# Down projection of the feed-forward layers: one Strassen level of seven products, activations stationary, sums made by adding DMAs, the stage in a fixed order

## The chip, the cores and the metric

The kernel is one program on one core of a Trainium2 chip. The metric is the device time of one execution in microseconds, as the median of several runs. The core's engines are called PE (matrix multiplication; PEld is its loading of the stationary operand), DVE, ACT and POOL; SP issues DMAs. POOL issues DMAs too, and all DMAs that add to what already stands in SBUF go through its queue.

## The reference

A two-layer encoder trunk on 512 tokens of width 1024: layer 0 mixes tokens by dilated window attention, layer 1 by gated linear attention (GLA), and each is followed by a feed-forward layer (SwiGLU) of hidden width 2816. The change is in the second product of that layer.

```python
def swiglu(h, w_gate_up, w_down):
    g, u = jnp.split(h @ w_gate_up, 2, axis=-1)
    return (jax.nn.silu(g) * u) @ w_down
...
for i in range(DEPTH):
    hn = rms_norm(h, attn_norm[i])
    ...
    h = h + mix.astype(h.dtype)
    h = h + swiglu(rms_norm(h, ffn_norm[i]), ffn_w_gate_up[i], ffn_w_down[i]).astype(h.dtype)
```

## The kernel before

All values are float32. Each operand of a product is split into a high part in a reduced format (`ACT` copies it) and the low remainder (`DVE` subtracts), and a product is three matmuls: high by high, high by low, low by high (`split`, L92; `mm3`, L106; `product`, L317). The residual h lies in eight tiles of 128 features by 512 tokens.

Gate-up (`gate_up`, L332) goes over six column chunks j, each of 512 gate and 512 up columns (the last 256), by one Strassen level in Winograd's form: seven products of half the size in each direction. Activations are stationary. The weight sums come from `forms` (L236): `load` on SP brings a block, and `add` (L249) issues an adding DMA on POOL. The chunk's results are turned by DVE (`turn`), stored to DRAM by `put` (L352, POOL; the last chunk on SP) in rows of tokens, and read back two chunks later as 22 tiles of 128 hidden features by 512 tokens (`get`, L361, SP). Eight of these tiles take the buffers of h, so h is stored to DRAM at j = 0 (L438) and read back at the end (L494).

The down projection (`down_part`, L471; `down`, L483) is the plain product: for each of eight output tiles m, 22 blocks of hidden features, weights stationary and the 512 tokens moving, three matmuls each. `weight` (L100) streams the weights of a tile in three pieces (1024, 1024 and 768 columns) through two `wf` buffers on SP, splits them, and PE takes 24 or 18 matmuls from each piece. The activations are split once (`halves`) and stay. As each m is done, L497 adds it to h, and `enter_norm` (L143) makes the operands of the next mixer. A little of m = 0 is started inside gate-up.

Outside `manual_schedule` the scheduler orders the instructions by program order and priorities. Each engine and each DMA queue then runs its own list in order, waiting at an instruction for the semaphores of what it needs. Buffers of a tag rotate (`BASE`, `FFN`, `MIX`: `wf` 2, `wh` 3, `wl` 3, `wA` 4, `wB` 2, `sh` 4, `sl` 4, `g` 7, `xs` 16); a new tile waits for the readers of the one whose place it takes. Behind the feed-forward layer of layer 0 comes GLA, whose first products (`linear`, L548, and the product of the gate ranks, L929) take the eight operands `self.x[k]` in order.

## Time and profile before

| | us |
|---|---|
| median of 3 runs | 1476.37 (1473.48 to 1476.51) |
| span of the profiled execution | 1475.3 |
| PE busy | 1449.8 (98% of the span) |
| DVE, ACT, POOL busy | 992.6, 756.1, 162.7 |
| down projection of layer 0, first to last matmul of L108 to L110 in one run | 785.6 to 904.8 |
| the same in layer 1 | 1352.2 to 1471.3 |
| loads of 512 KB, issue to landing: down weights on SP; gate-up weights on SP; gate-up adds and loads on POOL | 3.7; 5.0; 6.1 to 6.4 |
| moved by DMA | 219.61 MB, mean 149 GB/s |

The profiled execution's own time is given by its span, 1475.3 us from its first to its last instruction; the timed runs of the same kernel lie within 1.8 us of that. The views used are the page (busy times, 40 slices), the stretches (busy time of every engine between two times, with the DMA engines' share and rate), the timeline, the groups of instructions by line, and the DMA queues by stretch. q1 hardware_dynamic is what SP issues, q0 software_dynamic what POOL issues; the share is the time that the packets took on the 16 engines.

### The profile page before, as it was taken

Reading aid. Unit: us, or ns where it says so; the run is one execution under the profiler, and the core shown is the slowest. Engines: PE = TensorE matmul, PEld = TensorE weight load, DVE = VectorE, ACT = ScalarE, POOL = GpSimd, SP = SyncE. Lnnn points to the kernel's source line nnn. Section 1 sums busy time; section 2 is a strip of 40 time slices with the busy share of each in tenths; the row PEclk is TensorE's granted clock in tenths of the full one; section 3 lists DMA queues with packets and bytes.
Section 4 is the critical chain, followed back from the end, with each engine's and each line's share of the span. In section 5 each row is a group of like instructions: output and inputs, shape, how many; then the busy total and the mean of one; then the engine's idle time right before and its main releaser. Section 6 shows DMA issues by size and latency. Waiting matters only on the chain.

```text
span 1475.3 us, 20977 instructions
## 1 busy us (share of the span) xinstructions
PE 1449.8 (98%) x7742; PEld 1184.5 (80%) x7742; DVE 992.6 (67%) x1808; ACT 756.1 (51%) x1292; POOL 162.7 (11%) x272
## 2 busy tenths in 40 slices
PE   8999999999999999999999999999999999999998
PEld 6877878787778888877787887888888777778887
DVE  6586868778678669877676435756667876669322
ACT  6344444545566747655565324555745755556221
POOL 0001020101100021122230000000010122221000
PEclk9999999999999999999999999999999999999999
DMA  8644443454433365788887333212264788788431
GB/s 275 183 134 109 104 123 108 109 180 93 131 94 101 87 190 154 195 218 214 220 222 210 95 101 103 86 45 84 71 189 125 229 215 208 208 182 250 143 104 61
DMA packets 99831, 219.61 MB, mean 149 GB/s; under 512 B 15216, under 2 KB 42416, under 8 KB 99728
## 3 DMA queue, kind: packets, MB, share of 16 engines
q1 hardware_dynamic: 81072, 158.35, 34.5%
q0 software_dynamic: 18656, 59.91, 19.1%
q8 instruction: 61, 1.00, 0.3%
q14 instruction: 42, 0.34, 0.1%
HBM read 185.64 MB, written 19.99 MB: 139 GB/s over the span
## 4 chain that ended last, share of the span: by engine, by line
PE 66%; DVE 10%; issue 10%; DMA 7%; ACT 5%; POOL 1%; SPq 1%; DVEq 0%; POOLq 0%; ACTq 0%
PE ppp L110 9%; PE ppp L109 9%; PE ppp L108 9%; PE ppp L570 6%; PE ppp L571 6%; PE ppp L572 6%; PE ppp L329 3%; PE ppp L328 3%; PE ppp L330 3%; DVE wl L97 3%; DMA wA<-in_gate_up_last_dram 2%; DMA wB<-in_gate_up_dram 2%; PE po L701 2%; ACT wh L96 1%; PE ps L661 1%
## 5 line engine op out<-in xcount | busy, mean ns | idle before, releaser
L96 ACT ACTIVATE wh<-wf 128x1024 fp32r<-128x1024 f32 (+1 forms) x184 | 191.4, 1041 | 317.6 <-PE ppp L109 174.6
L97 DVE TENSOR_TENSOR wl<-wf,wh 128x1024 fp32r<-128x1024 f32 (+1 forms) x184 | 219.9, 1196 | 187.1 <-ACT wh L96 186.6
L570 PE MATMUL ppp<-wh,xs 128*128 128x512 f32 (+1 forms) x672 | 258.2, 385 | 7.2 <-ACT wh L96 5.7
L571 PE MATMUL ppp<-wl,xs 128*128 128x512 f32 (+1 forms) x672 | 257.3, 383 | 0.1
L572 PE MATMUL ppp<-wh,xs 128*128 128x512 f32 (+1 forms) x672 | 257.0, 383 | 0.0
L570 PEld LDWEIGHTS ppp<-wh,xs 128*128 128x128 f32 x672 | 126.8, 189 | 36.4 <-ACT wh L96 5.7
L572 PEld LDWEIGHTS ppp<-wh,xs 128*128 128x128 f32 x672 | 126.8, 189 | 25.6 <-issue 1.2
L571 PEld LDWEIGHTS ppp<-wl,xs 128*128 128x128 f32 x672 | 127.1, 189 | 24.8 <-DVE wl L97 0.9
L96 ACT ACTIVATE wh<-wA 128x1024 fp32r<-128x1024 f32 x88 | 93.2, 1059 | 73.4 <-PE ppp L330 27.3
L97 DVE TENSOR_TENSOR wl<-wA,wh 128x1024 fp32r<-128x1024 f32 x88 | 107.4, 1220 | 22.4 <-ACT wh L96 22.2
L329 PE MATMUL ppp<-wl,a 128*128 128x512 f32 (+1 forms) x288 | 108.1, 375 | 1.0 <-DVE wl L97 0.5
L328 PE MATMUL ppp<-wh,a 128*128 128x512 f32 (+1 forms) x288 | 108.4, 377 | 0.1
L108 PE MATMUL ppp<-xs,wh 128*128 128x512 f32 x272 | 106.5, 392 | 0.0
L109 PE MATMUL ppp<-xs,wh 128*128 128x512 f32 x272 | 106.5, 393 | 0.0
L110 PE MATMUL ppp<-xs,wl 128*128 128x512 f32 x272 | 106.0, 391 | 0.0
L330 PE MATMUL ppp<-wh,a 128*128 128x512 f32 (+1 forms) x288 | 105.5, 372 | 0.0
L97 DVE TENSOR_TENSOR wl<-wB,wh 128x1024 fp32r<-128x1024 f32 x38 | 46.5, 1223 | 78.2 <-ACT wh L96 78.2
L649 ACT ACTIVATE sm<-sm,st 128x160 f32<-128x160 f32 (+2 forms) x128 | 56.9, 446 | 43.5 <-DVE st L648 43.4
L329 PE MATMUL ppp<-wl,sh 128*128 128x512 f32 (+1 forms) x192 | 72.8, 379 | 4.6 <-DVE wl L97 4.4
L328 PE MATMUL ppp<-wh,sh 128*128 128x512 f32 (+1 forms) x192 | 71.9, 375 | 2.5 <-ACT g L379 1.8
L330 PE MATMUL ppp<-wh,sl 128*128 128x512 f32 (+1 forms) x192 | 71.6, 373 | 0.0
L251 POOL DMA_DIRECT2D wA<-in_gate_up_dram x44 | 38.5, 874 | 298.9 <-DVE wl L97 210.1
(319 smaller groups left out, 2949.0 us busy)
## 6 DMA issues: line engine op xcount, KB each, us to landing
wA<-in_gate_up_dram POOLq DMA_DIRECT2D x52, 512.0 KB, 6.1
wf<-in_down_dram SPq DMA_DIRECT2D x32, 512.0 KB, 3.7
wf<-in_gate_up_dram SPq DMA_DIRECT2D x24, 512.0 KB, 5.0
wf<-in_a_w_v_dram SPq DMA_DIRECT2D x20, 512.0 KB, 3.8
wB<-in_gate_up_dram POOLq DMA_DIRECT2D x20, 512.0 KB, 6.4
turned<-g POOLq DMA_DIRECT2D x80, 128.0 KB, 6.3
wf<-in_a_w_q_dram SPq DMA_DIRECT2D x16, 512.0 KB, 3.9
zq<-zs SPq DMA_DIRECT2D x128, 64.0 KB, 2.1
```

Source lines behind the costliest of these rows:

```text
L96: nc.scalar.activation(hi, src, AF.Copy)
L97: self.low = nc.vector.tensor_sub(lo, src, hi.bitcast(F32))
L108: mm(out, lhsT=wh, rhs=xh, start=start, stop=False)
L109: mm(out, lhsT=wh, rhs=xl, start=False, stop=False)
L110: self.multiplied = mm(out, lhsT=wl, rhs=xh, start=False, stop=stop)
L328: mm(a, lhsT=xh[:, tok], rhs=wh[:, f], start=start and k == 0, stop=False, skip_group_check=True)
L329: mm(a, lhsT=xh[:, tok], rhs=wl[:, f], start=False, stop=False, skip_group_check=True)
L330: self.multiplied = mm(a, lhsT=xl[:, tok], rhs=wh[:, f], start=False, stop=k == last, skip_group_check=True)
L570: mm(a, lhsT=xh, rhs=wh[:, f], start=k == 0, stop=False)
L571: mm(a, lhsT=xh, rhs=wl[:, f], start=False, stop=False)
L572: self.multiplied = mm(a, lhsT=xl, rhs=wh[:, f], start=False, stop=k == KT - 1)
L649: nc.scalar.activation(sm[:, w], sm[:, w], AF.Exp, bias=n, scale=-1.0, accum_out=l)
```

## The change

The down projection becomes seven products of half the size in each direction. A product has 256 tokens (two stationary tiles of 128), 512 output features (moving) and 1408 hidden features; the hidden features go in six blocks q, five of 256 and one of 128. A block's matmuls are an `item`: 2 token tiles x 2 (or 1) x 3. `ORDER` lists the 42 steps (product, q).

The weight operands are block 0, 1 and 3 of the down weights for products 1, 2 and 3, each streamed through `wf`; for products 5, 6 and 4 a chain tile (`wA`, `wB`) that starts as block 0 and has blocks 2, 3 and 1 added to it in turn; for product 7 block 3 plus block 2 (`sh`, `sl`). Loads are issued on SP, all additions on POOL as adding DMAs. The activation operands come from the turned results in DRAM in the same way: single quarters for 1, 2 and 4; the tile S (`g`), one quarter with three added in turn, for 5, 6 and 3; two quarters for 7. `gated` and `token_norm` give two of the four quarters the opposite sign in gate-up, by twice as many multiplications of half the width, so that all sums are additions. Every product's block of weights and of activations is split anew.

Products are collected in PSUM and in `g` tiles (`finished`), turned back by PE (`turned_back`: eight transposes into two banks and four DVE operations for a quarter of the output) and added to or subtracted from h, which now stays in SBUF. The output's last quarter comes after product 4; h 4 to 7 are complete earlier than h 0 to 3, and GLA's first products and the output take them first (`READY`). The stage stands in `manual_schedule`: `when` puts each DMA at a step, weights are split two steps ahead, activations four.

```diff
-        nc.vector.tensor_scalar(r[:, 4:8], r[:, 0:4], -1.0, None, op0=ALU.mult)
+        for half, sign in ((slice(0, 64), -1.0), (slice(64, P), 1.0)):
+            for c in (4, 8):
+                nc.vector.tensor_scalar(r[half, c:c + 4], r[half, 0:4], sign if c == 4 else -sign, None, op0=ALU.mult)
...
-        self.kept = self.dr.tile([KT, P, S], F32, name=f"h_dram_{layer}")
...
-        def get():
-            c = len(acts)
-            if c < min(4 * (j - 1), NH):
-                a = self.t("h") if c < KT else late[c - KT]
-                nc.sync.dma_start(a, turned[c].rearrange("b i a e -> (b i) (a e)"))
-                acts.append(a)
+        def fetch(p):
+            if j > 1:
+                self.raw[p, j - 2] = self.acts_block(self.t("xs", (P, 2, 256)), *self.FIRST[p], j - 2, nc.sync)
+
+        def gated(e, i, r, g):
+            half = width // 2
+            for n in range(2):
+                f = slice(n * half, (n + 1) * half)
+                col = 4 + 4 * n + i
+                DVE.scalar_tensor_tensor(e[:, f], e[:, f], r[:, col:col + 1], g[:, f], op0=ALU.mult, op1=ALU.mult)
...
-                DVE.scalar_tensor_tensor(e, e, R[:, 4 + i:5 + i], g1[:, i, 0:width], op0=ALU.mult, op1=ALU.mult)
+                gated(e, i, R, g1[:, i, 0:width])
...
-            if j == 0:
-                with self.tc.issue_after(self.added.ins):
-                    for m in range(KT):
-                        nc.gpsimd.dma_start(self.kept[m], self.h[m])
+            if j == 5:
+                self.down_start(layer)
...
+    FIRST = {1: (0, 0), 2: (0, 1)}
+    ORDER = ([(1, q) for q in range(5)] + [(2, q) for q in range(5)] + [(1, 5), (2, 5)]
+             + [(p, q) for p in (5, 6, 3, 7, 4) for q in range(6)])
+
+    def acts_block(self, tile, t, half, q, queue, add=False):
+        c = 4 * q + 2 * half if q < 5 else 20 + half
+        n = 2 if q < 5 else 1
+        src = self.turned_dram[c:c + n, :, :, 2 * t:2 * t + 2].rearrange("c b i a e -> (b i) c (a e)")
+        if add:
...
+    def down_block(self, tile, block, q, queue, add=False):
+        src = self.ins["down"][self.layer, block, q] if q < 5 else self.ins["down_last"][self.layer, block]
+        if add:
...
+    def split_weights(self, p, q):
+        w = self.wraw.pop((p, q)) if p in (1, 2, 3, 7) else self.chain[q]
+        c = 1024 if q < 5 else S
+        self.wpair[p, q] = self.split(w[:, 0:c], (P, c), "wh", "wl")
+
+    def split_acts(self, p, q):
+        nc = self.nc
+        n = 2 if q < 5 else 1
+        raw = self.raw.pop((p, q)) if p in (1, 2, 7, 4) else self.S[q]
+        raw = raw[:, 0:n]
+        hi, lo = (self.t("a", (P, 2, 256), F32R) for _ in range(2))
+        sign = -1.0 if p in (2, 6) else 1.0
+        nc.scalar.activation(hi[:, 0:n], raw, AF.Copy, scale=sign)
+        nc.vector.scalar_tensor_tensor(lo[:, 0:n], raw, sign, hi[:, 0:n].bitcast(F32), op0=ALU.mult, op1=ALU.subtract)
+        self.apair[p, q] = hi, lo
+
+    def stream(self, p, q):
+        self.wraw[p, q] = self.down_block(self.t("wf", (P, 1024)), {1: 0, 2: 1, 3: 3}[p], q, self.nc.sync)
+
...
+        for n in range(3):
+            self.stream(*order[n])
+        for n in range(3):
+            self.split_acts(*order[n])
+            if n < 2:
+                self.split_weights(*order[n])
+
+    def item(self, acc, p, q, tiles, start, stop):
+        mm = self.nc.tensor.matmul
+        (hi, lo), (wh, wl) = self.apair[p, q], self.wpair[p, q]
+        n = 2 if q < 5 else 1
+        for i in tiles:
+            tok = slice(i * P, (i + 1) * P)
+            for k in range(n):
+                f = slice(k * S, (k + 1) * S)
+                xh, xl = hi[:, k, tok], lo[:, k, tok]
+                mm(acc[i], lhsT=xh, rhs=wh[:, f], start=start and k == 0, stop=False, skip_group_check=True)
+                mm(acc[i], lhsT=xh, rhs=wl[:, f], start=False, stop=False, skip_group_check=True)
+                mm(acc[i], lhsT=xl, rhs=wh[:, f], start=False, stop=stop and k == n - 1, skip_group_check=True)
...
+        def chain_load(q):
+            self.chain[q] = self.down_block(self.t("wA" if q < 4 else "wB", (P, 1024)), 0, q, nc.sync)
+
+        def chain_add(q, block):
+            self.down_block(self.chain[q], block, q, nc.gpsimd, True)
+
+        def third_load(q):
+            self.wraw[7, q] = self.down_block(self.t("sh" if q < 4 else "sl", (P, 1024)), 3, q, nc.sync)
+
+        def third_add(q):
+            self.down_block(self.wraw[7, q], 2, q, nc.gpsimd, True)
...
+        def sum_load(q):
+            if q % 2 == 0:
+                rooms.append(self.t("g", (P, 2, 2, 256)))
+            self.S[q] = rooms[-1][:, q % 2]
+            self.acts_block(self.S[q], 1, 0, q, nc.gpsimd)
+
+        def sum_add(q, t, half):
+            self.acts_block(self.S[q], t, half, q, nc.gpsimd, True)
...
+        when(0, raw_load, 1, 4, 0, 0, nc.gpsimd)
+        when(2, raw_load, 2, 4, 0, 1, nc.gpsimd)
+        when(4, raw_load, 1, 5, 0, 0, nc.sync)
+        when(4, raw_load, 2, 5, 0, 1, nc.sync)
+        for n in range(3, len(order)):
+            if order[n][0] in (1, 2, 3):
+                when(n - 4, self.stream, *order[n])
+        for q in range(6):
+            when(at[5, q] - 10, chain_load, q)
+            when(at[5, q] - 8, chain_add, q, 2)
+            when(at[5, q] - 1, chain_add, q, 3)
+            when(at[6, q] - 1, chain_add, q, 1)
+            when(at[7, q] - 9, third_load, q)
+            when(at[7, q] - 7, third_add, q)
+            when(q + 1 if q < 4 else q + 3, sum_load, q)
+            when(q + 2 if q < 4 else q + 4, sum_add, q, 1, 1)
+            when(at[5, q] - 3, sum_add, q, 0, 0)
+            when(at[6, q] - 3, sum_add, q, 0, 1)
+            when(at[7, q] - 9, raw_load, 7, q, 0, 0, nc.sync)
+            when(at[7, q] - 7, raw_add, 7, q, 1, 0)
+            when(at[4, q] - 8, raw_load, 4, q, 1, 1, nc.sync)
+        splits = [[] for _ in order]
+        for n in range(2, len(order)):
+            splits[n - 2].append(partial(self.split_weights, *order[n]))
+        for n in range(3, len(order)):
+            splits[max(n - (2 if order[n] == (1, 4) else 4), 0)].append(partial(self.split_acts, *order[n]))
...
+        def turned_back(tile, half, t, sign):
+
+            for b, tag in enumerate("to"):
+                bank = self.p(tag)
+                for e in range(2):
+                    for i in range(2):
+                        c = slice((2 * b + e) * P, (2 * b + e + 1) * P)
+                        nc.tensor.transpose(bank[:, (2 * e + i) * P:(2 * e + i + 1) * P], tile[:, i, c], self.ident)
+                for e in range(2):
+                    h = view(self.h[4 * half + 2 * b + e])[:, 2 * t:2 * t + 2]
+                    part = bank[:, 2 * e * P:2 * (e + 1) * P].rearrange("p (a g j) -> p a g j", a=2, j=32)
+                    op = ALU.add if sign > 0 else ALU.subtract
+                    DVE.tensor_tensor(out=h, in0=h, in1=part, op=op)
+
...
-        for m in range(KT):
-            if m > 0:
-                ps = self.p("pp")
-            self.down_part(ps, layer, m, 2 if m == 0 else 0, NH, pairs)
-            h = self.t("h")
-            nc.sync.dma_start(h, self.kept[m])
-            self.h[m] = h
-            order = "p (g a j) -> p a g j"
-            nc.vector.tensor_add(h.rearrange(order, a=4, j=32), ps.rearrange("p (a g j) -> p a g j", a=4, j=32),
-                                 h.rearrange(order, a=4, j=32))
...
-                self.enter_norm(m, self.h[m], self.cols[:, col_next + m:col_next + m + 1])
+                self.x[m] = self.gained(self.h[m], self.cols[:, col_next + m:col_next + m + 1])
+                self.add_square(m == 4, self.h[m])
...
+            elif p == 7:
+                for i in range(2):
+                    DVE.tensor_add(kept[5][:, i], b1[i], kept[5][:, i])
+            else:
+                kept[4] = copy()
+                ACT(kept[4][:, 0], b1[0], AF.Copy)
+                DVE.tensor_copy(kept[4][:, 1], b1[1])
+
+        tails = {at[5, 2]: lambda: turned_back(kept[1], 0, 0, 1), at[7, 2]: lambda: turned_back(kept[6], 1, 0, -1),
+                 at[4, 2]: lambda: turned_back(kept[5], 1, 1, -1)}
+        for m in range(4, KT):
+            tails[at[4, m - 2 if m < 7 else 5]] = partial(lambda m, was: (was and was(), enter(m)), m, tails.get(at[4, m - 2 if m < 7 else 5]))
+        with self.tc.manual_schedule():
+            for n, (p, q) in enumerate(order):
+                for step in plan[n] + splits[n]:
+                    step()
+                if n in tails:
+                    tails[n]()
+                first = q == 0 and p in (1, 2, 5)
+                if p in (7, 4) and q == 5:
+                    for i in range(2):
+                        self.item(acc[p], p, 4, [i], False, False)
+                        self.item(acc[p], p, 5, [i], False, True)
+                elif p not in (7, 4) or q < 4:
+                    self.item(acc[p], p, q, range(2), first, q == 5)
+                if q == 5:
+                    finished(p)
+            turned_back(kept[4], 0, 1, 1)
+            for m in range(4):
+                enter(m)
 
     def attn_consts(self):
         nc, t = self.nc, self.t
@@ -548,10 +708,12 @@
     def linear(self, dram):
         wh, wl = self.weight(dram, KT * P)
...
-        for k in range(KT):
+        for n, k in enumerate(self.READY):
             c = slice(k * P, (k + 1) * P)
-            self.mm3(ps, wh[:, c], wl[:, c], *self.x[k], k == 0, k == KT - 1)
+            self.mm3(ps, wh[:, c], wl[:, c], *self.x[k], n == 0, n == KT - 1)
         return ps
+
...
-    a["down"] = np.stack([blocks(w) for w in ffn_w_down])
+    d = ffn_w_down[:, :2560].reshape(2, 5, 2, 2, P, 2, 512).transpose(0, 5, 2, 1, 4, 3, 6)
+    a["down"] = np.ascontiguousarray(d.reshape(2, 4, 5, P, 1024))
+    d = ffn_w_down[:, 2560:].reshape(2, 2, P, 2, 512).transpose(0, 3, 1, 2, 4)
+    a["down_last"] = np.ascontiguousarray(d.reshape(2, 4, P, 512))
```

On POOL's queue, at the end of gate-up of layer 0, before (turned is the DRAM copy of the results, in_gate_up the weights of layer 1's gate-up):

```order
L251 DMA wA_7524<-in_gate_up_last_dram 128x1024
L359 DMA turned_5961<-g_7480 32x8x128 x4
L359 DMA turned_5961<-g_7481 32x8x128 x4
L246 DMA wA_10399<-in_gate_up_dram 128x1024
L246 DMA wA_10401<-in_gate_up_dram 128x1024
```

The same place in the changed kernel, the first rows of the down projection (g_7799 and g_7858 are S tiles, wA the chain; L459 and L467 load, L457 and L465 add):

```order
L459 DMA xs_7771<-turned_5946 128x2x256
L459 DMA g_7799<-turned_5946 128x2x256
L459 DMA xs_7821<-turned_5946 128x2x256
L457 DMA g_7799<-turned_5946 128x2x256
...
L459 DMA g_7858<-turned_5946 128x2x256
L465 DMA wA_7825<-in_down_dram 128x1024
L457 DMA g_7858<-turned_5946 128x2x256
```

POOL, which had nothing to issue for the down projection, now has 56 DMAs there per layer, and an S addition stands directly behind the load into the same tile. On SP's queue, in the down projection of layer 0, before:

```order
L103 DMA wf_7940<-in_down_dram 128x1024
L359 DMA turned_5961<-g_7741 32x8x128 x4
L103 DMA wf_7970<-in_down_dram 128x768
L103 DMA wf_8005<-in_down_dram 128x1024
L365 DMA xs_5959<-turned_5961 128x512
L365 DMA xs_5960<-turned_5961 128x512
L103 DMA wf_8035<-in_down_dram 128x1024
```

and now:

```order
L467 DMA wf_7773<-in_down_dram 128x1024
L359 DMA turned_5946<-g_7755 32x8x128 x4
L467 DMA wf_7775<-in_down_dram 128x1024
L467 DMA wf_7797<-in_down_dram 128x1024
L467 DMA wf_7823<-in_down_dram 128x1024
L467 DMA wA_7825<-in_down_dram 128x1024
L467 DMA wf_7853<-in_down_dram 128x1024
L467 DMA wA_7855<-in_down_dram 128x1024
L459 DMA xs_7880<-turned_5946 128x256
L459 DMA xs_7882<-turned_5946 128x256
```

The loads of the chain now stand between the streams of products 1 and 2, behind the last four stores of `put`.

More of the change, by code (lines that the diff above doesn't have):

```diff
@@ L232, in swiglu @@
             out_projection()
-            self.gate_up(layer, acts)
-            self.down(layer, acts, col_next)
+            self.gate_up(layer)
+            self.down(layer, col_next)
     def forms(self, dram, own, ahead=0):
@@ L471, in down_part @@
-    def down_part(self, ps, layer, m, k, end, pairs):
-        for k0, kn in ((0, 8), (8, 8), (16, 6)):
-            if k0 <= k < min(end, k0 + kn):
-                if k == k0:
-                    self.down_w = self.weight(self.ins["down"][layer, m, :, k0 * P:(k0 + kn) * P], kn * P)
-                wh, wl = self.down_w
-                while k < min(end, k0 + kn):
-                    c = slice((k - k0) * P, (k - k0 + 1) * P)
-                    self.mm3(ps, wh[:, c], wl[:, c], *pairs[k], k == 0, k == NH - 1)
-                    k += 1
-        return ps, pairs
@@ new lines @@
+    ORDER = ([(1, q) for q in range(5)] + [(2, q) for q in range(5)] + [(1, 5), (2, 5)]
[5 more added lines that the diff above has]
+        if add:
+            queue.dma_start(tile[:, 0:n], src, accum_op=ALU.add)
+        else:
+            queue.dma_start(tile[:, 0:n], src)
+        return tile
@@ L928, in gla_body @@
         pz = self.p("pp")
-        for k in range(KT):
+        for n, k in enumerate(self.READY):
             xh, xl = self.x[k]
-            if k > 0:
+            if n > 0:
                 nc.tensor.matmul(pz[0:32], lhsT=wzs[:, k, 0:32], rhs=xl, start=False, stop=False)
-            nc.tensor.matmul(pz[0:64], lhsT=wzs[:, k], rhs=xh, start=k == 0, stop=k == KT - 1)
-            if k == 0:
+            nc.tensor.matmul(pz[0:64], lhsT=wzs[:, k], rhs=xh, start=n == 0, stop=n == KT - 1)
+            if n == 0:
                 nc.tensor.matmul(pz[0:32], lhsT=wzs[:, k, 0:32], rhs=xl, start=False, stop=False)
@@ L1237, in build @@
             k.swiglu(1, None, k.out_gla)
-        for m in range(KT):
+        for m in (4, 5, 6, 7, 0, 1, 2, 3):
             nc.sync.dma_start(out[m], k.h[m])
```

103 lines of the change are left out of this document (63 added, 40 removed).

## The prediction, made before the result was known

> **What bounds the kernel now.** The page comes first: the share of busy time, then the DMA row of the 40 slices. TensorE (PE) is busy for nearly all of the span; the DMA engines are three to five tenths busy in most slices, but seven to eight tenths in the two feed-forward stages.
>
> ```profile
> PE 1449.8 (98%) x7742; PEld 1184.5 (80%) x7742; DVE 992.6 (67%) x1808; ACT 756.1 (51%) x1292; POOL 162.7 (11%) x272
> ...
> DMA  8644443454433365788887333212264788788431
> ```
>
> The view of stretches says which part of the feed-forward stage that is. Columns: us, busy time of PE, PEld, DVE, ACT and POOL with counts, granted clock, DMA share, GB/s. The first two rows are gate-up, the third the down projection.
>
> ```profile
> 720.00:760.00 40.00, 39.93 (x174) 32.04 (x173) 28.64 (x32) 23.85 (x31) 11.74 (x16) 1.00 0.86 206
> ...
> 1320.00:1350.00 30.00, 28.90 (x192) 25.32 (x191) 28.72 (x41) 21.56 (x36) 6.82 (x11) 1.00 0.89 263
> ...
> 840.00:870.00 30.00, 30.00 (x134) 24.86 (x133) 10.66 (x12) 8.43 (x10) 0.00 (x0) 1.00 0.35 98
> ```
>
> So gate-up, which is already a Strassen level fed by adding DMAs, keeps PE full with the DMA engines at 0.86 to 0.89 of their time: little is left there. The down projection uses a third of them. It is bounded by PE alone, as the timeline shows (start, duration, engine, line):
>
> ```profile
> 785.62 0.40 PE L108 MATMUL ppp<-xs,wh 128*128 128x512 f32 x1
> ...
> 904.53 0.39 PE L110 MATMUL ppp<-g,wl 128*128 128x512 f32 x1
> ...
> 904.96 0.69 DVE L497 TENSOR_TENSOR h<-ppp,h 128x512 f32<-128x512 f32 x1 [1.94 <-PE ppp L110]
> ...
> 1352.17 0.40 PE L108 MATMUL ppp<-xs,wh 128*128 128x512 f32 x1
> ...
> 1471.04 0.39 PE L110 MATMUL ppp<-g,wl 128*128 128x512 f32 x1
> ```
>
> From the first to the last of these 525 matmuls are 524 steps in 118.91 us, 0.227 us each, with no hole; layer 1 takes 118.87. Three more run earlier inside gate-up. With the last matmul and the addition of L497 the stage takes 120 us per layer, and that is what the change replaces.
>
> **What it removes on PE.** 8 x 22 x 3 = 528 matmuls per layer become 7 x 11 x 2 x 3 = 462. 462 x 0.227 = 104.9 us, so 15.0 us less per layer. It adds 32 transposes per layer; the nearest row has three in a run:
>
> ```profile
> 938.88 0.49 PE L1025 MATMUL pt<-ident,wa 128*128 128x128 f32 x3
> ```
>
> 0.49 / 3 is 0.16 us each at most: 5.2 us in all, 1.3 of it in the tail. PE alone would need 104.9 + 5.2, some 110 us per layer.
>
> **What it adds on the DMA engines.** I count in passes: one pass over a weight quarter is 5.5 blocks of 512 KB, 2.88 MB; one over an activation quarter is 5.5 blocks of 256 KB, 1.44 MB. Weights are loaded in five passes (products 1, 2, 3, the chain, the third sum) and added in four (three on the chain, one on the third sum). Activations are loaded in five passes (1, 2, S, 7, 4) and added in four (three on S, one for 7). Of these, three weight blocks and eight activation blocks are issued in gate-up. In the stage are left: weight loads 12.85 MB, weight adds 11.53, activation adds 5.77, activation loads 3.15 on SP and 1.97 on POOL, the last store of `put` 0.52: 35.8 MB, where 120 us at the 98 GB/s of the third stretch above are 12. What a megabyte costs stands in the DMA view by stretch (packets, MB, share of the 16 engines); the rows are of 640 to 680 us (two), 744 to 749 (adds alone), 709 to 713 (mostly POOL's stores in 512-byte runs), 764 to 768 (loads in 2 KB runs) and 410 to 470 (mostly 512-byte runs).
>
> ```profile
> q0 software_dynamic: 1248, 4.20, 52.4%
> q1 hardware_dynamic: 1630, 4.57, 31.5%
> ...
> q0 software_dynamic: 273, 0.99, 105.8%
> ...
> q0 software_dynamic: 344, 0.98, 96.7%
> ...
> q1 hardware_dynamic: 473, 1.04, 82.7%
> ...
> q1 hardware_dynamic: 5331, 4.73, 31.9%
> ```
>
> Loads: 4.57 MB in 0.315 x 40 us, 363 GB/s. Adds: 0.99 MB in 1.058 x 5 us, 187 GB/s; the mixed row gives 4.20 MB in 21.0 us, 200; I take 190. The two shares of a stretch never sum to much over 100%, so adds and loads take turns on the engines: their times sum. Adds in 1 KB runs, which the activations need, do not occur. Upper end 200, as in the mixed row; lower end 130, half of a 1 KB load if that runs at 260 (between 314 from 764 to 768 and 247 from 410 to 470), since a 4 KB add takes about twice a 4 KB load. I take 175, nearer the top, because POOL's stores in 512-byte runs still moved 253 GB/s. Plain activation loads: 260 to 363, I take 300; POOL's likewise.
>
> Per layer: weight adds 11.53/0.190 = 60.7; activation adds 5.77/0.175 = 33.0; weight loads 12.85/0.363 = 35.4; activation loads 3.15/0.3 + 1.97/0.3 = 17.1; `put` 0.52/0.253 = 2.1. Sum **148 us of all 16 engines**, against 110 us of PE. The ends: 57.7 + 28.9 + 35.4 + 14.1 + 1.4 = 138, and 61.7 + 44.4 + 35.4 + 19.7 + 2.1 = 163. The down projection is to become bounded by transfers.
>
> The Trainium skill, "DMA: Bandwidth & Descriptors", section "Anatomy of one DMA", has a DMA take about 2.0 us plus its bytes over 436e3 per us; by that, an estimate, 35.8 MB would take 82 us and PE would stay the bound, rival (1) below. The rows above, 363 for loads and 187 for adds, disagree, and they decide.
>
> **From transfers to the stage.** The last add feeds the last block of product 7; behind it PE still has 12 matmuls of 7 and all 66 of product 4: 78 x 0.227 = 17.7 us. Then the tail: a copy, eight transposes (1.3), four additions of 256 columns behind each other, and in layer 0 splits of the last four h tiles.
>
> ```profile
> L379 ACT ACTIVATE g<-ppp 128x512 f32<-128x512 f32 x60 | 35.3, 590 | 25.8 <-PE ppp L330 25.2
> ...
> L191 DVE TENSOR_TENSOR sl<-g,sh 128x256 fp32r<-128x256 f32 x16 | 6.6, 421 | 0.2
> ```
>
> 0.6 + 1.3 + 4 x 0.42 = 3.6; in layer 0 the splits come on top, but PE has matmuls on h 4 to 7 ready (`READY`), so 4 for both. Gaps: POOL issues in order, and each S add stands right behind the load of its own tile, so early on POOL waits out a landing several times, and the chain adds that product 5 needs queue behind it. On SP the chain loads stand behind streams that wait for one of two `wf` buffers; on ACT and DVE a split that waits for its block holds up the splits of later blocks, and PE waits for those. Zero would need perfect overlap; 0.86 as in gate-up would make it 24 us. But there the engines paused because PE had been served; here they are behind, so I take 7, near the lower end. Stage: 148 + 17.7 + 4 + 7 = 177 us, +57 per layer. The profiled span is 1475.3 and the median 1476.37, so 1.1 us lie outside: 1475.3 + 114 + 1.1 = **1590 us**.
>
> **Costed at nothing.** `gated` splits each multiplication of L421 and L445 into two.
>
> ```profile
> L421 DVE SCALAR_TENSOR_TENSOR g<-g,Rc,g 128x512 f32<-128x512 f32 x20 | 14.1, 747 | 1.9 <-ACT g L393 1.9
> ```
>
> Two of 256 columns at the 0.42 of L191 against 0.75 is +0.1 us, 24 per layer, 2.4 us of DVE, hidden since DVE was busy 28.64 of 40 us in gate-up; without that cover, 2.4 us per layer. The h tiles stay in SBUF: 2 MB of stores and 2 of loads leave gate-up, worth at most the 1.1 us in 30 that PE idled from 1320 to 1350. The new splits, 38.5 blocks, take ACT 1.06 + 0.6 and DVE 1.22 + 0.75 us per block, some 64 and 76 us, beside 177.
>
> **Rivals.** (1) *PE stays the bound*, the faster side. Were adds as quick as loads and the two queues served beside each other, PE sets the stage: 104.9 + 3.9 + 4 = 113, -7 per layer, 1462. It decides from the point at which all transfers fit in 91 us (113 less the 22 behind the last add), 393 GB/s. Against it: loads without adds reach 363.
>
> (2) *Landing latency.* With enough bandwidth, the two `wf` buffers still limit products 1, 2 and 3: a buffer is held from issue until DVE has split it.
>
> ```profile
> wf<-in_gate_up_dram SPq DMA_DIRECT2D x24, 512.0 KB, 5.0
> ...
> L96 ACT ACTIVATE wh<-wf 128x1024 fp32r<-128x1024 f32 x168 | 177.8, 1059 | 279.1 <-PE ppp L109 138.4 <-PE ppp L572 56.1 <-DMA wf<-in_a_w_k_dram 24.6
> L97 DVE TENSOR_TENSOR wl<-wf,wh 128x1024 fp32r<-128x1024 f32 x168 | 204.5, 1218 | 185.2 <-ACT wh L96 184.8
> ```
>
> 5.0 + 1.06 + 1.22 over two buffers is 3.64 us per block against 12 x 0.227 = 2.72 of PE: 15 blocks x 0.92 = 13.8, stage 127, 1490. It needs the same cheap adds, so it holds only if my add price is far off.
>
> (3) *PE cools down.* At the start of the kernel matmuls begin 0.43 us apart, later 0.23:
>
> ```profile
> 7.18 0.63 PE L572 MATMUL ppp<-wh,xs 128*128 128x512 f32 x1
> 7.61 0.63 PE L570 MATMUL ppp<-wh,xs 128*128 128x512 f32 x1
> ...
> 9.71 0.40 PE L570 MATMUL ppp<-wh,xs 128*128 128x512 f32 x1
> 9.94 0.39 PE L571 MATMUL ppp<-wl,xs 128*128 128x512 f32 x1
> ```
>
> If the waits put PE back to that pace throughout, 462 x 0.43 = 199 us, stage at least 206, 1648 or more. The Trainium skill, "TensorE: Matmul & The Clock Gate", section "HAM oscillation", says that idle gaps over about 3.4 us bring this about; my mean gap is only (177 - 110)/38.5 = 1.7 us, so by that rule a few items run cold, not all. No row here shows PE starved in mid-run.
>
> (4) *Nothing moves*: the costs cancel within 0.2%, about what a measurement of this kernel tells from no change.
>
> **How the numbers follow.** The transfer bound 0.80: its ends are 138 + 22 with nothing in gaps, 160, 1556; and 163 + 22 + 24, 209, 1654. (3) 0.07, (2) 0.06, (1) 0.05, (4) 0.02. The range of 1520 to 1660 holds the first case, with some room below for transfers that start before gate-up ends, and leaves out the others. Faster 0.05, same 0.02, slower 0.93.
>
> **What would show it.** Right: a DMA share over 0.85 through both down stages, POOL's adds landing some 8 us or more after issue, PE idle in products 5, 6 and 3 behind splits of chain blocks that wait for adds, and PE full again only in product 4. Wrong: a share under 0.8 while PE is full (1 or 2), or matmuls 0.43 us apart in mid-stage (3). Adds at over 300 GB/s would break the forecast.

## The result, and the profile after

The changed kernel took **1585.54 us** (median of 4 runs, 1584.07 to 1587.70) against 1476.16 us of the kernel before beside it: a ratio of 1.0741, 95% interval 1.0721 to 1.0760. The forecast was 1590, the range 1520 to 1660. The profiled execution has a span of 1585.9 us.

The page of the changed kernel, parts 1 and 2 (busy time and share of the span; 40 slices of 40 us):

```profile
PE 1480.7 (93%) x7674; PEld 1187.1 (75%) x7674; DVE 1070.3 (67%) x1968; ACT 815.5 (51%) x1382; POOL 264.0 (17%) x368
...
PEclk9999999999999999999999799999999999999978
DMA  8534444544433657688799953221465878879992
```

In the two down projections the DMA row of before has 333 (layer 0) and 431 (layer 1, the end of the span); now both have 999. PE has 68 instructions fewer and 31 us more of busy time: a busy PE here is partly a slower one, since the granted clock fell in just those slices. (A matmul counts as busy until its modelled end, so a few slow ones add up.)

The view of stretches of layer 0's down projection (us, busy PE, PEld, DVE, ACT, POOL with counts, granted clock, DMA share, GB/s):

```profile
787.00:815.00 28.00, 24.51 (x104) 18.15 (x103) 14.47 (x20) 12.12 (x16) 7.68 (x8) 1.00 0.94 262
815.00:830.00 15.00, 11.16 (x33) 8.14 (x34) 5.63 (x8) 5.76 (x9) 4.64 (x5) 0.77 1.08 299
830.00:847.00 17.00, 11.76 (x52) 8.96 (x51) 7.98 (x10) 5.70 (x9) 7.21 (x10) 0.95 1.02 246
847.00:875.00 28.00, 24.64 (x91) 18.16 (x90) 15.74 (x22) 14.02 (x20) 19.53 (x19) 0.91 1.12 197
875.00:911.00 36.00, 23.36 (x66) 16.00 (x64) 8.74 (x11) 8.84 (x13) 10.12 (x10) 0.76 1.09 262
911.00:935.00 24.00, 19.00 (x72) 13.74 (x72) 14.14 (x21) 10.35 (x15) 3.88 (x4) 0.93 0.95 215
935.00:958.00 23.00, 19.98 (x86) 15.98 (x85) 16.14 (x25) 11.66 (x18) 0.00 (x0) 0.93 0.08 24
```

For 148 us the DMA share stands at 0.94 to 1.12, and in the last 23 us, product 4, it is 0.08. Between 875 and 911 PE issued 66 matmuls in 36 us, where 66 at 0.227 take 15. No engine but the DMA engines is full: this is a stage bounded by transfers, followed by the work behind the last one. The same stretch in the DMA view and in the view of waits (us in total, times, longest):

```profile
q0 software_dynamic: 9841, 18.48, 58.4%
q1 hardware_dynamic: 8840, 18.06, 31.9%
...
wA<-in_down_dram POOLq DMA_DIRECT2D x12, 512.0 KB, 12.8
...
ACT wh L96 <- DMA wf<-in_down_dram: 33.9, 9, 9.0
POOL g L457 <- DMA g<-turned: 31.2, 5, 10.1
...
PEld ps L511 <- ACT wh L96: 17.8, 5, 4.7
```

Of 171 us, 58.4% are 99.9 us for the 18.48 MB of POOL's queue (adds, and 1.15 MB of loads), 185 GB/s, and 31.9% are 54.5 us for the 18.06 MB of the others, 331 GB/s: 154 us of all engines. An add of a chain block landed 12.8 us after its issue. PE waits for splits, the splits for transfers, and no further.

### The profile page after: what moved, and what is told of

It reads as the page before. It is cut to its first block, busy times and chain, and to the rows that moved or that the text cites. A ratio compares the mean times of both kernels' runs of the same rounds, so it can differ in the third digit from the quotient of the medians.

```text
span 1585.9 us, 21320 instructions
## 1 busy us (share of the span) xinstructions
PE 1480.7 (93%) x7674; PEld 1187.1 (75%) x7674; DVE 1070.3 (67%) x1968; ACT 815.5 (51%) x1382; POOL 264.0 (17%) x368
## 3 DMA queue, kind: packets, MB, share of 16 engines
q1 hardware_dynamic: 85104, 158.88, 31.9%
## 4 chain that ended last, share of the span: by engine, by line
PE 54%; DMA 17%; DVE 11%; issue 9%; ACT 6%; POOL 2%; SPq 0%; DVEq 0%; ACTq 0%; POOLq 0%
PE ppp L732 7%; PE ppp L733 7%; PE ppp L734 6%; PE ppp L330 4%; PE ppp L329 4%; PE ppp L331 4%; DMA wf<-in_down_dram 3%; PE ppp L108 3%; PE ppp L109 3%; PE ppp L110 3%; DVE wl L97 3%; DMA xs<-turned 3%; ACT wh L96 2%; DMA wB<-in_gate_up_dram 2%; PE po L863 2%
## 5 line engine op out<-in xcount | busy, mean ns | idle before, releaser
L97 DVE TENSOR_TENSOR wl<-wf,wh 128x1024 fp32r<-128x1024 f32 (+1 forms) x172 | 206.2, 1200 | 174.6 <-ACT wh L96 174.3
L96 ACT ACTIVATE wh<-wf 128x1024 fp32r<-128x1024 f32 (+1 forms) x172 | 179.4, 1043 | 268.0 <-DMA wf<-in_down_dram 65.4
L96 ACT ACTIVATE wh<-wA 128x1024 fp32r<-128x1024 f32 x112 | 118.4, 1058 | 107.7 <-PE ppp L331 48.6
L97 DVE TENSOR_TENSOR wl<-wA,wh 128x1024 fp32r<-128x1024 f32 x112 | 136.7, 1220 | 53.4 <-ACT wh L96 52.9
L329 PE MATMUL ppp<-wh,a 128*128 128x512 f32 (+1 forms) x288 | 110.2, 383 | 8.4 <-ACT g L383 8.4
L97 DVE TENSOR_TENSOR wl<-wB,wh 128x1024 fp32r<-128x1024 f32 (+1 forms) x50 | 57.9, 1159 | 84.2 <-ACT wh L96 84.2
L511 PE MATMUL ppp<-wh,a 128*128 128x512 f32 x220 | 92.1, 419 | 16.3 <-ACT wh L96 9.2
L512 PE MATMUL ppp<-wl,a 128*128 128x512 f32 x220 | 93.9, 427 | 14.3 <-DVE wl L97 14.2
L108 PE MATMUL ppp<-xs,wh 128*128 128x512 f32 x256 | 100.2, 393 | 0.1
L109 PE MATMUL ppp<-xs,wh 128*128 128x512 f32 x256 | 100.2, 392 | 0.0
L110 PE MATMUL ppp<-xs,wl 128*128 128x512 f32 x256 | 99.8, 392 | 0.0
L513 PE MATMUL ppp<-wh,a 128*128 128x512 f32 x220 | 90.4, 411 | 0.2
L96 ACT ACTIVATE wh<-wB 128x1024 fp32r<-128x1024 f32 (+1 forms) x50 | 50.4, 1007 | 60.8 <-DMA wB<-in_gate_up_dram 33.3
```

The costliest lines, as they stand in the source:

```text
L96: nc.scalar.activation(hi, src, AF.Copy)
L97: self.low = nc.vector.tensor_sub(lo, src, hi.bitcast(F32))
L108: mm(out, lhsT=wh, rhs=xh, start=start, stop=False)
L109: mm(out, lhsT=wh, rhs=xl, start=False, stop=False)
L110: self.multiplied = mm(out, lhsT=wl, rhs=xh, start=False, stop=stop)
L329: mm(a, lhsT=xh[:, tok], rhs=wh[:, f], start=start and k == 0, stop=False, skip_group_check=True)
```

## The experiments

The down stage is measured from the start of the last gate-up matmul of L329, two places ahead of the very last one (L328 in the kernel before), to the start of the last matmul of product 4, in the kernel before of m = 7. "DMA" is the sum of the two queues' shares over layer 0's stage, in us of 16 engines.

| kernel | us | ratio to before, 95% | stage, layer 0 and 1 | DMA |
|---|---|---|---|---|
| before | 1476.2 | 1 | 119, 119 | 46 |
| changed | 1585.5 | 1.0741, 1.0721 to 1.0760 | 169.9, 168.8 | 154 |
| no adds | 1483.6 | 1.0053, 1.0018 to 1.0088 | 116.6, 120.0 | 56 |
| adds as plain loads | 1513.2 | 1.0247, 1.0199 to 1.0294 | 132.1, 134.1 | 102 |
| no weight adds | 1502.8 | 1.0176, 1.0119 to 1.0233 | 128.8, 129.6 | 95 |
| no activation adds | 1525.7 | 1.0331, 1.0293 to 1.0369 | 138.2, 137.3 | 115 |
| more stream buffers | 1580.9 | 1.0705, 1.0659 to 1.0751 | 166.0, 166.1 | |
| activation sums on VectorE | 1567.3 | 1.0609, 1.0563 to 1.0655 | 158.4, 160.5 | |
| weight sums on VectorE | 1573.9 | 1.0655, 1.0605 to 1.0706 | 162.8, 164.8 | |
| all sums on VectorE | 1626.8 | 1.1011, 1.0965 to 1.1057 | 189.3, 189.9 | |
| the same, one item ahead | 1541.7 | 1.0432, 1.0407 to 1.0456 | 144.9, 147.3 | |
| first splits late | 1576.3 | 1.0675, 1.0653 to 1.0697 | 168.4, 169.4 | |
| no adds, first splits late | 1473.1 | 0.9976, 0.9964 to 0.9988 | 118.0, 118.7 | |
| one item ahead, splits late | 1530.7 | 1.0373, 1.0350 to 1.0396 | 146.4, 148.4 | |

**Is it the adds?** Four kernels, all edits in `acts_block` and `down_block`. First, no adding DMA at all:

```diff
         if add:
-            queue.dma_start(tile[:, 0:n], src, accum_op=ALU.add)
+            pass
...
         if add:
-            queue.dma_start(tile[:, 0:src.shape[1]], src, accum_op=ALU.add)
+            pass
```

> The sums of the Strassen operands are left out (no adding DMA is issued; the plain loads, products, and the combination of the products stay). Theory of the sum of transfer times: what is left in a down stage is about 61 us of 16 engines, less than the 110 us that PE needs for 462 matmuls at 0.227 us, so PE is the bound: stage 113 to 118 us, kernel about 1470 us (1455 to 1485). Rival, the landing latency of loads into the two `wf` buffers: about 1490 us. Rival, the splits and the cooled-down PE (matmuls 0.43 us apart after each wait) as such: the splits and their order are all still there, so over 1560 us.

1483.6 us: within the range, 14 above its middle. The stage is PE's again (116.6 and 120.0 us), with the order and all splits as they were, so the splits and the order alone do not make the loss. The rest of the 8 us over the kernel before is taken up below.

Second, the same DMAs and bytes, without the adding:

```diff
-            queue.dma_start(tile[:, 0:n], src, accum_op=ALU.add)
+            queue.dma_start(tile[:, 0:n], src)
...
-            queue.dma_start(tile[:, 0:src.shape[1]], src, accum_op=ALU.add)
+            queue.dma_start(tile[:, 0:src.shape[1]], src)
```

> Every adding DMA is issued as a plain load of the same bytes on the same queue (so the operands hold the last block that was loaded, not the sum). Same count of DMAs, same bytes, same waits. Theory of the sum: the price of an adding byte is what matters (174 to 185 GB/s against about 340 for a plain load): 36.65 MB / 340 GB/s = 108 us, and some 22 us behind the last transfer: stage about 130 us, kernel about 1500 us (1475 to 1520). Rivals (landing latency, the splits' order, volume of bytes whatever the kind): little change, 1560 to 1590 us.

1513.2 us, inside the range, and its DMA view of 787 to 920 us:

```profile
q1 hardware_dynamic: 8833, 18.04, 38.6%
q0 software_dynamic: 5360, 18.48, 38.4%
```

POOL's 18.48 MB took 0.384 x 133 = 51.1 us here and 99.9 us when they added: **the adding itself costs nearly as much as the load**. Of some 109 us that the change lost, 72 go with it. One thing changes beside the adding: the loads of the activations move in larger packets than their adds did (last section). For the weights the packets are of 4 KB either way (2 KB for the adds of the last block), so there the size is no rival: 11.56 MB are 59.5 us as adds (worked out below) and, by an estimate at the 18.48 / 51.1 = 362 GB/s of this queue here, 32 us as loads.

Third and fourth, one kind of add left out at a time (the edit of the first, in `down_block` alone and in `acts_block` alone):

> The adding DMAs of the weights are left out (24 of 512 KB for each layer), those of the activations stay. Theory of the sum: 11.5 MB at about 185 GB/s = 62 us go, 93 us of transfers are left for each layer, less than PE's 110: about 1478 us (1465 to 1500). Rival, the chain blocks of products 5, 6, 3 whose activations wait for adds of 1 KB runs: over 1530 us.

> The adding DMAs of the activations are left out (40 of 256 KB in each layer's stage by the issue rows, 5.8 MB with those of the other sizes), those of the weights stay. Theory of the sum: 33 us of transfers go, 122 us are left and some 22 behind them: stage about 144 us, kernel about 1527 us (1510 to 1545). Rival, the weights' waits (`wh` split behind the `wf` transfer, 65 us of idle on ScalarE, are what counts, the activations come in their shade): within 15 us of the changed kernel, 1570 to 1590.

1502.8 and 1525.7 us. The fourth is as the sum has it: 115 + 22 behind the last transfer = 137, measured 138.2. The third missed its range (1465 to 1500): the stage takes 129 us, 10 more than before. I had compared 93 us of transfers with PE's 110 and forgotten that product 4 comes behind them. (The 40 DMAs of 256 KB in the expectation of the fourth are those of both layers; one stage adds 20 of 256 KB and four of 128, the 5.8 MB.) The view of stretches of that kernel:

```profile
845.00:860.00 15.00, 15.00 (x68) 12.43 (x67) 10.07 (x12) 9.18 (x15) 4.53 (x4) 1.00 0.70 134
860.00:875.00 15.00, 13.55 (x58) 10.36 (x57) 6.75 (x9) 6.75 (x10) 3.58 (x3) 1.00 1.06 334
...
890.00:905.00 15.00, 11.98 (x41) 9.31 (x40) 9.53 (x14) 6.00 (x8) 0.00 (x0) 0.77 0.00 1
```

PE is the bound from 845 to 860, the DMA engines are from 860 to 875, and from 890 on hardly a byte moves. So the rule for the stage is transfers + 22 us where that is well above PE's 117 (115: 137 against 138; 154: 176 against 170), and some 8 to 12 us more than either bound where the two come near each other (102: 124 against 132; 95: 117 against 129), where they change places within the stage. That this makes the excess was read from these rows and not tried; in the last row the granted clock of 0.77 has a part in it too. The adds' costs don't add either: activations alone +12 us of stage, weights alone +22, both +53.

**Is it landing latency?** (rival 2)

```diff
-        self.wraw[p, q] = self.down_block(self.t("wf", (P, 1024)), {1: 0, 2: 1, 3: 3}[p], q, self.nc.sync)
+        n = self.ORDER.index((p, q))
+        self.wraw[p, q] = self.down_block(self.t("sl" if n > 2 and n % 2 else "wf", (P, 1024)), {1: 0, 2: 1, 3: 3}[p], q, self.nc.sync)
```

> The blocks that are streamed for products 1, 2 and 3 go alternately into the `wf` and the spare `sl` buffers from the fourth on, so a load no longer waits for the split two blocks back. Same transfers, same bytes. Theory of the sum: ScalarE's 65 us of idle before the splits of `wf` only show that the 16 engines are full, so nothing changes: 1585 us (1578 to 1592). Rival, two `wf` buffers and the landing latency hold the stream back: about 13 us for each layer come back, about 1558 us (1545 to 1570).

1580.9 us, the transfers' case (4.6 us less, inside its range). Its waits show how a wait changes its name when the engines are full:

```profile
ACT wh L96 <- DMA wf<-in_down_dram: 6.3, 1, 6.3
...
ACT a L482 <- DMA g<-turned: 28.4, 11, 12.0
ACT a L482 <- DMA xs<-turned: 24.9, 6, 9.2
```

ScalarE waits 6.3 us for `wf` instead of 33.9 and 53 us for activations instead of 32 (18.9 and 12.7 there): the streams that came sooner pushed the activations back.

**Can VectorE make the sums?** First the activations' sums: the add becomes a plain load into a spare tile, added ahead of the split.

```diff
+        more = self.due.pop((p if p == 7 else "S" if p in (5, 6, 3) else None, q), None)
+        if more is not None:
+            nc.vector.tensor_add(raw, raw, more[:, 0:n])
         hi, lo = (self.t("a", (P, 2, 256), F32R) for _ in range(2))
...
         def sum_add(q, t, half):
-            self.acts_block(self.S[q], t, half, q, nc.gpsimd, True)
+            self.due["S", q] = self.acts_block(self.t("xs", (P, 2, 256)), t, half, q, nc.gpsimd)
```

> The sums of the activations are made on VectorE: each adding DMA becomes a plain load of the same bytes into a spare `xs` tile, and an addition (0.68 us for 128x512) stands ahead of the split. Theory of the sum: the activations' adding transfers, some 35 us for each layer by the two kernels without adds, become plain loads of some 17 us: 17 to 19 us for each layer go, about 1550 us (1540 to 1560). Rival, the waits on VectorE's queue grow by as much as the transfers shrink (VectorE gets 15 us more for each layer): 1575 us or more.

Then the weights' sums alone (a 512 KB tile of `sl` for each, `tensor_add` ahead of the split of that block; the last two blocks of the third sum, which had `sl`, go to `wf` and are loaded two steps later), and both:

```diff
     def split_weights(self, p, q):
...
+        if (p, q) in self.wdue:
+            self.nc.vector.tensor_add(w[:, 0:c], w[:, 0:c], self.wdue.pop((p, q))[:, 0:c])
...
-            when(at[5, q] - 8, chain_add, q, 2)
-            when(at[5, q] - 1, chain_add, q, 3)
-            when(at[6, q] - 1, chain_add, q, 1)
+            when(at[5, q] - 5, other_load, 5, q, 2)
+            when(at[6, q] - 5, other_load, 6, q, 3)
+            when(at[4, q] - 5, other_load, 4, q, 1)
```

> The sums of the weights alone on VectorE, those of the activations stay with the adding DMAs. Theory of the sum: 11.5 MB go at the price of a plain load (32 us) and not of an add (60 us), 28 us for each layer go: about 1529 us (1515 to 1545). Rival, VectorE's 30 us more for each layer stand in the chain of the splits: 1560 us or more.

> All sums on VectorE, those of the weights too (24 additions of 1.23 us for each layer, from a tile that a plain load fills some three steps ahead). Theory of the sum: transfers as in the kernel with plain loads in place of the adds (1513 us), and VectorE gets 45 us more for each layer, so some 125 of a stage of 135 us: about 1525 us (1510 to 1545). Rival, VectorE becomes the bound of the stage or its queue makes PE wait: 1550 us or more.

1567.3, 1573.9 and 1626.8 us: half of the expected gain, a fifth, and a loss of 41. The first lies between theory and rival, in the other two the rivals hold. Of the kernel with all sums on VectorE, one of five stretches from 830 to 905 us, in which VectorE is busy 9.5 to 10.5 of 15 us and the DMA share is 0.37 to 0.64 (this one has the lowest):

```profile
860.00:875.00 15.00, 9.26 (x26) 5.80 (x24) 10.42 (x16) 4.01 (x5) 4.75 (x8) 0.79 0.37 120
```

DMA share 0.37, VectorE 10.4 of 15 us, ScalarE 4.0, and 26 matmuls on PE where 66 would have room: **no engine is full**. What fills the time are hand-overs: VectorE adds, ScalarE makes the high part of that sum, VectorE, waiting for it in order, the low part, and only then the next addition. The view of waits of the stage (787 to 990 us) has these hand-overs:

```profile
DVE wl L97 <- ACT wh L96: 52.8, 37, 5.7
...
ACT a L487 <- DVE g L484: 31.1, 18, 1.9
...
DVE a L488 <- ACT a L487: 15.9, 24, 0.7
```

VectorE waits 68.7 us in all for the high parts and not once for a load. If so, an order in which each addition stands one item ahead should free it, at the same work (the plain loads move one step ahead with it):

```diff
+        for n in range(3, len(order)):
+            splits[n - 3].append(partial(self.sum_weights, *order[n]))
+        for n in range(5, len(order)):
+            splits[n - 5].append(partial(self.sum_acts, *order[n]))
         for n in range(2, len(order)):
             splits[n - 2].append(partial(self.split_weights, *order[n]))
```

> All sums on VectorE as in the kernel that came out at 1627 us, but each addition stands one item ahead of the split that reads it, and its plain load one step earlier, so that VectorE adds while ScalarE makes the high part. Theory of the ping-pong: there the DMA engines were only 0.4 to 0.5 busy in mid-stage, and a block's addition, high part and low part (1.23, 1.05 and 1.22 us, and 2 us for its activations) ran one after the other over two engines; with the addition ahead the stage falls to VectorE's own work, some 125 us and 10 to 15 us of fill and tail: about 1530 us (1510 to 1555). Rival, VectorE's amount of work itself is the bound and the order does not matter: 1600 us or more.

1541.7 us, 85 less than the same instructions in the other order. The earlier loads can hardly have made it, since VectorE had not waited for them; they were not moved alone. Two stretches of it:

```profile
830.00:845.00 15.00, 12.85 (x53) 9.80 (x52) 15.00 (x20) 6.86 (x10) 5.03 (x9) 0.89 0.79 284
845.00:860.00 15.00, 11.55 (x49) 8.54 (x48) 15.00 (x22) 7.17 (x11) 7.38 (x12) 1.00 0.75 241
```

In these 30 us VectorE is full, 15.00 of 15, and the DMA engines are not. Over the stage VectorE is busy 117 of 144 us; with the additions right ahead of the splits it was 120 of 189. The sums have moved much of the bound to another engine, and the stage is still 26 to 28 us longer than the 119 of before.

**What is lost outside the stage.** In the kernel without adds 5 us are lost between the two down stages: 452.8 us from the end of the first to the start of the second, 447.3 before. The timeline of the changed kernel shows where (start, duration, engine, line; in brackets the idle time before and its releaser), first ScalarE, then PE:

```profile
1260.53 0.63 ACT L482 ACTIVATE a<-xs 128x512 fp32r<-128x512 f32 x1 [4.45 <-DMA xs<-turned]
1261.07 0.58 ACT L383 ACTIVATE g<-ppp 128x512 f32<-128x512 f32 x1
...
1261.70 0.74 PE L329 MATMUL ppp<-wh,a 128*128 128x512 f32 x1 [4.00 <-ACT g L383]
```

L482 is the first operand split of the down projection. Outside the stage's fixed order the scheduler had put it into the middle of gate-up, ahead of a copy of L383 that frees a PSUM buffer for PE, and its operand was still on the way. Layer 0 has the same (4.86 us on ScalarE at 640, 4.4 on PE). The edit:

```diff
             if j == 5:
-                self.down_start(layer)
+                with self.tc.issue_after(silu.ins):
+                    self.down_start(layer)
```

> The changed kernel with one edit: the first operand splits of the down projection may not be placed ahead of the last gate's activation, so ScalarE no longer stands 4.45 us in mid gate-up for the load of `xs` (place 546 of its list before, 631 now). Theory: PE's wait of 4 us there in layer 1 goes, and up to 2 us in layer 0: about 1581 us (1578 to 1583). Rival, the wait only moves to the next slot where ScalarE or PE is held: no change, 1585 us (1584 to 1588).

> The kernel without any adding DMA (the sums left out) and with the first operand splits placed late. Theory: the 5 us that the kernel without adds loses between its two down stages are this wait: about 1479 us (1475 to 1482), still no gain over the kernel before. Rival, the loss between the stages has another cause: 1483 us (1482 to 1486).

1576.3 and 1473.1 us: 9.3 and 10.6 us less, both below their ranges, some twice the expected gain. PE's two waits, 4.4 and 4.0 us, are gone from the trace, and so is what came behind them, which I had left out: PE at half its clock. The same stretch, first of the changed kernel, then of this one:

```profile
640.60:647.50 6.90, 6.06 (x15) 4.82 (x15) 3.12 (x4) 2.22 (x4) 0.93 (x1) 0.51 0.60 159
...
640.60:647.50 6.90, 6.90 (x31) 5.68 (x31) 6.17 (x10) 3.60 (x5) 1.79 (x2) 1.00 0.93 227
```

In layer 1 of the changed kernel the clock is 0.50 from 1261.8 to 1265.2. In the two places some 20 matmuls start 0.43 us apart, where 0.227 is the pace: 4.6 us, 13.0 with the waits, of which the two gate-ups keep 11.5 (223.1 and 225.9 us from first to last matmul, 216.9 and 220.6 with the splits late). With this the change without its sums is 0.24% faster than before, so even free sums would have bought almost nothing. What it gains lies in gate-up: the last matmul of L329 in layer 0 starts at 781.0 us there, that of L328 before at 785.3. Last, the two edits that helped, together:

> The two edits that helped, together: all sums on VectorE one item ahead (1541.7 us), and the first operand splits late (9 us off the changed kernel, 10 off the one without adds). Theory: they lie in different stages and add up: about 1532 us (1527 to 1537), still slower than before, since VectorE with some 125 us of work for each layer is now beside the transfers the bound of a stage that took 119 us before. Rival, the early splits cost nothing where VectorE is the bound, since the time comes back in the stage: 1540 us or more.

1530.7 us: they add up, to the fastest form of the change that was found, 3.7% slower than before.

## Why the prediction was right, step by step

*PE bound before, 15.0 us saved per layer.* The saving is there (462 matmuls) but mostly does not arrive: without adds and with the splits late the stage takes 118.0 and 118.7 us against 119. "PE alone would need some 110" left out what PE waits for inside the stage even when transfers are ample: short waits for low parts (up to 0.8 us each), a stretch of 3.4 us at half the clock, and ahead of it 3.0 us at the start of product 4, whose first matmul waits until VectorE has taken product 7's result out of the same PSUM buffers:

```profile
886.94 0.47 PE L511 MATMUL ppp<-wh,a 128*128 128x512 f32 x1 [3.02 <-DVE g L633]
```

That row is of the kernel without adds; the changed kernel has the same wait at 940.01.

*Transfers, 148 us.* Measured 154, 4% more. By differences of the queue's time: weight adds 11.56 MB in 59.5 us (no activation adds less no adds), 194 GB/s where I took 190; activation adds 5.80 MB in 36.9 us (no weight adds less no adds), 157 where I took 175, within the ends of 130 and 200. So the price of adding, on which everything rested, was read rightly from gate-up's rows for the weights and some 11% too cheap for the activations, and the kernel with plain loads shows it to be the cause. By the Trainium skill, "DMA: Bandwidth & Descriptors", section "Anatomy of one DMA", 36.65 MB would be some 84 us, an estimate; the plain loads took 102 and the adds with their loads 154, so its price per byte does not cover an adding DMA.

*From transfers to the stage.* Here two terms were off and cancelled. "Gaps" of 7 us: there were none; the transfers of 154 us were through in some 148, because shares ran to 1.12 where I had said that they never sum to much over 100%. "Behind the last add 17.7 us": some 22, from the drop of the DMA share at 935 to 957.4; the 3.0 us wait above and some eight matmuls 0.43 us apart after it (8 x 0.2 = 1.6) are the difference. Stage and tail, to the last addition to h: 174 in layer 0 and 172 in layer 1, for 177 forecast.

*Costed at nothing: the new splits.* This step failed. I had set their 64 and 76 us beside the 177 of the stage, but five of each layer's are in gate-up, the first ahead of work that PE needs: 9 to 11 us in all, shown by moving them. They hid a gain beside them: with the splits late and no adds gate-up is 4.3 us shorter than before in layer 0 and 4.6 in layer 1. The stores and loads of h that leave it, which I had put at 1.1 us in 30 at most, may be the cause; that was not tried alone. That the forecast is only 4 us off is luck: in the traces of before and after, some 5 us are lost net outside the two stages, and the stages came out 3 and 5 us shorter than forecast.

*Rivals.* (1) PE the bound, 1462: refuted as it stood, and its own price was too low; without any adds 1483.6. (2) Landing latency: refuted by the stream buffers. (3) The cooled PE: I had written that matmuls 0.43 us apart in mid-stage would speak for it, and they are there, at a granted clock of 0.76 and 0.77. Some 60 of the 462 in layer 0 are so slow. Where the DMA share is 1.08 beside them they should cost nothing, since PE would only have waited longer; the kernel without activation adds has stretches at 0.77 too, and its stage is the transfers' sum, but no run changes the clock alone. Where transfers are not the bound they do cost: 1.6 us in product 4 of layer 0 and 4.6 us in gate-up behind the early splits, which I had not looked for there. "No row here shows PE starved in mid-run" was too short a look: the kernel before has a wait of 2.71 us up to 425.4 us, and a granted clock of 0.50 for the 3.4 us behind it. Of the signs, the DMA share, the landing times and the waits of products 5, 6 and 3 came as written; that PE is full again only in product 4 is right but for its start.

The whole loss, each kernel against the before of its own runs: change without adds, splits late -4.4 us; splits early +12.7; the adds' bytes as plain loads +29.6; the adding itself +71.5; together the 109.4. (The befores differ by up to 2.2 us: by the medians alone, the early splits are 10.6.)

## What to carry to other kernels

An adding DMA saves an engine's work, but here it took about twice the DMA time of the load, so sums go to it only where the sixteen engines have that time to spare; add up the transfers of the *new* stage at rates read from a stage that already does such adds, and add the work behind the last transfer. When sums move to an engine that also stands in a relay (add, high part, low part), put them one item ahead in its list: the same instructions, with their loads one step earlier, took 85 us less. And look where a scheduler puts the first instructions of a stage with a fixed order: one early split in each layer cost nearly a tenth of the whole loss.

## What the runs showed of the hardware

- The 16 engines' times summed to more than the stretch: 1.12 with both queues, and 1.11 with adds alone (847 to 870 us, first row below: 4.45 MB in 25.5 us of engine time within 23). What lies over another there was not settled.

```profile
q0 software_dynamic: 2550, 4.45, 111.0%
```

- Activation adds went out in about 1 KB packets (6020 packets more for 5.80 MB, no weight adds against no adds), while plain loads of the same blocks on the same queue took 1528 for 5.77 MB (plain loads against no activation adds), 3.8 KB each. Whether the small packets or the adding set their 157 GB/s against the weights' 194 was not separated.
- In the traces' clock records the granted clock is 1.00 or 0.50 and nothing between, and all changes in mid-run lie on one grid of 3.41 us steps in each trace (changed kernel: 0.50 from 640.56 for 6.83 us, from 1261.79 for 3.41, from 1514.38 for 13.65). So it mattered where in the grid a wait fell. One wait of 3.02 us, in the same place, cooled PE in one layer and not in the other (kernel without adds: matmuls 0.23 us apart after it in layer 0, 0.43 from 1458.74 on in layer 1). In layer 0 it lay across two steps, in which PE was busy 2.11 and 1.66 us of 3.40 (first row: the second of them). In layer 1 it lay within one, with 0.52, and the next step has half the clock (second and third row):

```profile
885.20:888.60 3.40, 1.66 (x7) 1.42 (x8) 3.40 (x6) 1.12 (x2) 0.00 (x0) 1.00 0.00 0
...
1455.30:1458.70 3.40, 0.52 (x2) 0.49 (x3) 3.10 (x5) 2.25 (x4) 0.00 (x0) 1.00 0.01 2
1458.70:1462.10 3.40, 3.40 (x9) 2.67 (x8) 1.66 (x2) 0.00 (x0) 0.00 (x0) 0.50 0.02 5
```

The Trainium skill, "TensorE: Matmul & The Clock Gate", section "What's actually happening", has a free-running window of about 3.4 us decide this; the grid and the rows agree with that, but the window did not have to be wholly idle. By the section "HAM oscillation" of that page of the Trainium skill the gap must be over some 3.4 us. The waits of 3.02 us here and of 2.71 us in the kernel before were shorter and cooled PE, so the measurement decides.
